# A hybrid decoder block in float32: the order of work in the second pair's mixers, and more weight sums split ahead

## The chip, the cores and the metric

One core of a Trainium2 chip. The time is device microseconds of one execution on that core, from runs of the same program; a profile of one further execution shows where it went. TensorE (PE) multiplies, VectorE (DVE), ScalarE (ACT) and GpSimd (POOL) do the rest, and DMAs are issued from the queues of SyncE (SP), ACT and POOL.

## What is computed

One layer of a decoder trunk on x of 2048 rows by 1024 columns, all in float32. The reference, cut to what matters:

```python
h = rmsnorm(x, norm_mix_g)
u = h @ w_in                       # 1024 -> 3*512 + 2*1024 columns
gate_b, gate_c, v, x_r, g = split(u)
y_conv = gate_b * causal_dwconv(gate_c * v, conv_w)          # 3 taps
xr = causal_dwconv(x_r, rnn_conv_w) + rnn_conv_b             # 4 taps
y_rnn = rg_lru(xr, w_a, b_a, w_x, b_x, lru_lambda) * gelu(g) # gates by 64x64 blocks, scan over rows
y = concat[rmsnorm(y_conv, g_norm_conv), rmsnorm(y_rnn, g_norm_rnn)]
x = x + y @ w_out                  # 1536 -> 1024
h = rmsnorm(x, norm_mlp_g)
x = x + relu(h @ w_mlp_in)**2 @ w_mlp_out                    # 1024 -> 4096 -> 1024
out = rmsnorm(x, final_norm_g)
```

## The kernel before, in words

**Pairs of blocks.** The 2048 rows are four blocks of 512. They are worked in two pairs, one after the other: mixers (the projection `w_in`, the convolutions and the recurrence), then the output projection `w_out`, then the MLP's two products, which the page calls `up` and `dn`. A pair's mixers of the first pair (`mixers_plain`) multiply plainly. Those of the second pair (`mixers_blocks`) and both MLP products (`Up`, `Down`) treat the two blocks, two halves of the inner size and two halves of the columns as a 2 by 2 matrix product and do it in seven block products in place of eight, with sums of quarters as operands. The seven products are numbered 1 to 7 and run in `ORDER = (1, 2, 6, 5, 7, 3, 4)`. Products 1, 2 and 4 take a quarter of the weights as it is; 7, 5, 6 and 3 take a sum of quarters.

**Splits.** Each operand is split in a high and a low part of the type fp32r (`round_off`: ACT casts the high part, DVE subtracts it from the source for the low part, lines 172 and 173), and a product is three passes: high by high, high by low, low by high. A block product of the mixers is 24 matmuls of 128x512 (line 885, written `in`), one of `Down` is 24 as well (line 1187, `dn`).

**The second pair's mixers.** The columns of `w_in` are seven groups, run in the order `SEQUENCE = (0, 4, 1, 5, 2, 6, 3)`. Groups 0 to 3 (`InLru`) hold the recurrence's input and its gate g, 4 and 5 (`InConv`) the convolution's c and v, 6 (`InGate`) its b. The list `seq` of 49 products starts with products 1 and 2 of the groups 0 and 4, then the other five of group 0 (n = 4 to 8) and of group 4 (n = 9 to 13), then seven each of the groups 1, 5, 2, 6 and 3 (n = 14 to 48). For each n the loop fetches the weights of a product three or four places ahead, splits (`prepare`) those that were fetched raw two places ahead, multiplies, empties PSUM (`drain`), and then does one step of the recurrence of the LRU group before, if one is due:

- step 0: the gate products of the group's first unit (`psri`, line 518), and the second unit's convolution and split (`xr`, `xr_hi`, `xr_lo`);
- step 1: the first unit's scan: a tanh and an exponential on ACT (lines 541 and 542), DVE work, a square root on ACT, the scan itself on DVE (line 548), and on POOL the copy of its last state (line 549);
- step 2: the second unit's gate products, the first unit's output;
- steps 3 and 4: the second unit's scan and its output.

`STEPS` says after which product of a group each step runs: `{1: 0, 6: 1, 5: 2, 7: 3, 3: 4}` for the groups 5 and 6, and `STEPS2` for group 4, whose products 1 and 2 run early. Group 3's steps run between the row tiles of `w_out` (`between`).

**Weight sums ahead.** The first pair's mixers store each quarter that stands as it is already split (`d_ws`, a high and a low part of 512 KB each), and each sum of quarters unsplit (`d_wk`, 512 KB). In the first pair's `Down` loop, which has 56 products (n = 0 to 55), `split_sums(k)` loads one such sum (`wk`), splits it and stores both parts. It runs at every third product, 16 times, which covers the four sums of each of the groups 0 to 3. The sums of the groups 4, 5 and 6 stay raw: in the second pair's mixers the SP queue loads each, and `prepare` splits it on ACT and DVE. What was split ahead comes through the POOL queue as two loads (`wr`, line 857) straight into two tiles that the matmuls read.

**Tiles and queues.** Weights, LRU units and raws of the mixers share one pool of 15 tiles of 128x1024 (`wtile`), most other data one of 23 (`temp`); a tile is reused when its last reader is done. PSUM has four tiles. The order on PE is the program's. The order on ACT, DVE, POOL and SP is chosen by a planner that walks the program by priority with modelled times; every queue then runs in that fixed order. `tc.issue_after(ins)` puts the instructions traced under it that are on the same engine as `ins` behind `ins` in this order.

**Between the stages.** `take` loads and splits the next unit of `w_in` or `w_out`. In group 3, `load_unit` already asks for the first `w_out` unit (`oA0`) at product 7 and the second (`oA1`) at product 3; both are split when `w_out` starts. `stats` makes the sums of squares of a whole pair with one-column matmuls into PSUM (`sps`, line 646), block by block, and the inverse roots from them. The last row tiles of the second pair are finished in an order written out by hand for PE, ACT and DVE: `end_tile` gives the tail of a tile, of which `scale()` is run after the next tile's addition and squares.

Of the kernel before, what the change touches and what calls it, by code (L numbers as in the profile page):

```python
# [8 lines left out]
F32 = mybir.dt.float32  # L9
# [5 lines left out]
P = 128  # L15
# [22 lines left out]
LEADW = 2  # L38
ORDER = (1, 2, 6, 5, 7, 3, 4)
STEPS = {1: 0, 6: 1, 5: 2, 7: 3, 3: 4}  # L40
STEPS2 = {6: 0, 5: 1, 7: 2, 3: 3, 4: 4}
GROUPS = [("x%d" % p, COL_X + 256 * p, "g%d" % p, COL_G + 256 * p) for p in range(4)]
GROUPS += [("c%d" % p, COL_C + 256 * p, "v%d" % p, COL_V + 256 * p) for p in range(2)]
GROUPS += [("b0", COL_B, "b1", COL_B + 256)]
# [17 lines left out]
def block_kernel(  # L62
# [46 lines left out]
    def psum(name, shape=(P, 2, TB)):  # L109
        return psp.tile(list(shape), F32, tag="ps", name=name)  # L110
# [12 lines left out]
    def small(name):  # L123
        return sp.tile([P, NT], F32, tag=name, name=name)

    def load(dst, src):
        queued[0] = nc.sync.dma_start(dst, src).ins

# [40 lines left out]
    cursor = [0]  # L169

    def round_off(hi, src, lo):
        nc.scalar.copy(hi, src)  # L172
        latest[0] = V.tensor_tensor(lo, src, hi.bitcast(F32), SUB).ins  # L173

    latest = [None]

    def split_new(src, new, nm):
        shape = list(src.shape)
# [139 lines left out]
    nc.scalar.activation(warm, ones[:, 0:1], AF.Sqrt)  # L318

    def rstd_of(dst, v, n):  # L320
        a = small("rs_a")[:, :n]
        s = small("rs_s")[:, :n]
        q = small("rs_q")[:, :n]
        V.tensor_scalar(a, v, 1.0 / D, EPS, MUL, ADD)
        root = nc.scalar.activation(s, a, AF.Sqrt)
        V.reciprocal(s, s)
        if n == 1:
            V.scalar_tensor_tensor(q, s, a, s, MUL, MUL)
        else:
            V.tensor_mul(q, s, s)  # L330
            V.tensor_mul(q, q, a)
        V.tensor_scalar(q, q, -0.5, 1.5, MUL, ADD)
        V.tensor_mul(dst, s, q)
        return root.ins
# [303 lines left out]
        return refill("u", d, lambda nm, shape: wide(nm))  # L638

    def stats(acc, n, nm):  # L640
        res = []
        for blk in range(2):
            ps = psum("sps", (P, NT))
            for t in range(NT):
                a = blk * TB + t * P
                nc.tensor.matmul(  # L646
                    ps[:, t : t + 1], acc[:, a : a + P], ones[:, 0:1], start=True, stop=True
                )
            ss = small("ys_" + nm)
            V.tensor_scalar(ss, ps, float(D) / n, None, MUL)  # L650
            r = small("yr_" + nm)
            rstd_of(r, ss, NT)
            res.append(r)
        return res

    def split_y(y, nm, c0):
        hi = temp("y_hi", dt=F32R)
# [25 lines left out]
            kept[n, i] = spill("wk", t, nc.gpsimd)  # L683

    def split_sums(k):
        key = (k // 4, (7, 5, 6, 3)[k % 4])
        t = refill("wk", kept[key])
        kept[key] = [spill_r("ws", r, nc.gpsimd) for r in split_new(t, temp, "w")]

# [286 lines left out]
    def mixers_blocks(H, more):  # L976
        G = [InLru(n) for n in range(4)] + [InConv(n) for n in (4, 5)] + [InGate(6)]
        two = SEQUENCE[:2]
        seq = [(n, i) for n in two for i in ORDER[:2]]
        seq += [(n, i) for n in two for i in ORDER[2:]]  # L980
        seq += [(n, i) for n in SEQUENCE[2:] for i in ORDER]
        behind = {b: a for a, b in zip(SEQUENCE, SEQUENCE[1:]) if a < 4}
        mix = Mix()

        def step(p, k):
            if k == 0:
                p.units[0].gate(p.gw)
                p.units[1].conv(p.xin)
            elif k == 1:
                p.units[0].scan()  # L990
            elif k == 2:
                p.units[1].gate(p.gw)
                mix.out(p.units[0], p.g)
            elif k == 3:
                p.units[1].scan()
            elif k == 4:
                mix.out(p.units[1], p.g)

        for n in range(-FETCHW, len(seq)):
            for m, sums in ((n + FETCHW, True), (n + FETCHW - 1, False)):  # L1000
                if 0 <= m < len(seq) and (seq[m][0] > 3 and seq[m][1] not in (1, 2, 4)) == sums:
                    G[seq[m][0]].fetch(seq[m][1])
            m = n + LEADW
            if 0 <= m < len(seq):
                G[seq[m][0]].prepare(seq[m][1])
            if n < 0:
                continue
            s, i = seq[n]
            if s == 6 and i == 1:
                G[6].us = [G[4].u, G[5].u]  # L1010
            G[s].multiply(i, H)
            G[s].drain(i)
            more(n)
            if s in behind:
                k = (STEPS2 if s == two[1] else STEPS).get(i)
                if k is not None:
                    step(G[behind[s]], k)
            if s == 6 and i in (3, 4):
                mix.conv(G[6].u0 if i == 3 else G[6].u1)
            if s == 3 and i == 6:  # L1020
                rA = stats(mix.acc["A"], 512, "A")
            if s == 3 and i in (7, 3):
                load_unit(cursor[0] + (i == 3))
            if s == 3 and i == 3:
                fetched = [fetch_y(mix.ys["A"], q, 0) for q in range(2)]

        def between(t):
            if t == 0:
                step(G[3], 0)
                step(G[3], 1)  # L1030
            if t == 1:
                step(G[3], 2)
                step(G[3], 3)
            if t == 3:
                step(G[3], 4)

        return mix, rA, conv_operands(fetched), between
# [197 lines left out]
    def end_tile(b, t, gfin, ss, final):  # L1235
        rs = small("rs")[:, 0:1]
        a = small("rs_a")[:, 0:1]
        V.scalar_tensor_tensor(a, ss[:, 0:1], 1.0 / D, ss[:, 1:2], MUL, ADD)
        root_of(rs, a)
        r0 = b * TB + t * P  # L1240
        x0, x1 = (x_half(b, t, i) for i in range(2))

        def scale():
            nc.scalar.activation(x1, x1, AF.Copy, scale=rs)  # L1244
            (nc.scalar if final else nc.sync).dma_start(outf[r0 : r0 + P, HALF[1]], x1)
            V.scalar_tensor_tensor(x0, x0, rs, gfin[:, HALF[0]], MUL, MUL)  # L1246
            nc.sync.dma_start(outf[r0 : r0 + P, HALF[0]], x0)

        return scale

    def finish(b):
        gfin = gain(final_norm_g)
# [112 lines left out]
    for b in range(0, NB, 2):  # L1365
# [99 lines left out]
        with tc.manual_schedule(engines={nc.tensor.engine}):  # L1465
# [52 lines left out]
            for n in range(len(dseq) - (0 if more else 2)):  # L1518
# [14 lines left out]
                if (i, a) == (4, 0):  # L1533
                    finish(b)
                if more:
                    if n % 3 == 2 and n < 48:
                        split_sums(n // 3)
                    if (i, a) == (5, 0):
                        load_xt(2)
                        ops2 = Operands()  # L1540
                    if (i, a) == (6, 1):
                        diags = [diagonal(rs_next[:, k, :], NT) for k in range(2)]
                    if (i, a) == (6, 4):
                        bcs = [temp("bcs", (P, TB)) for _ in range(2)]
                        for k in range(2):
                            nc.scalar.copy(bcs[k], spread(rs_next[:, k, :], NT, diags[k]))
                    if i == 7 and a < 4:
                        r0 = [xtt[2, q] for q in range(4)]
                        scale_rows(r0[a], 2 * a, bcs[0], 2)
                        ops2.first_two(1 + a // 2, r0[a])  # L1550
                    if (i, a) == (7, 4):
                        load_xt(3)
                    if i == 3 and a < 4:
                        r1 = [xtt[3, q] for q in range(4)]
                        scale_rows(r1[a], 2 * a, bcs[1], 2)
                    if i == 3 and a in (5, 6):
                        q = a - 5
                        V.tensor_tensor(r0[q], r1[q], r0[q], SUB)
                    if i == 4 and a in (0, 1):
                        if a == 0:  # L1560
                            T2 = [temp("T2") for _ in range(2)]
                        V.tensor_tensor(T2[a], r1[2 + a], r0[a], SUB)
                        V.tensor_tensor(r0[2 + a], r0[2 + a], T2[a], SUB)
                        V.tensor_tensor(r1[a], r1[2 + a], r1[a], SUB)
                    if i == 4 and a == 3:
                        ops2.put(ops2.begin(6), T2)
                    if i == 4 and a == 5:
                        ops2.put(ops2.begin(5), r0[:2])
# [8 lines left out]
        if not more:  # L1577
            order = (0, 2, 1, 3)
            with tc.manual_schedule(
# [3 lines left out]
                for t in order:  # L1583
                    for i, a in dseq[-2:]:
                        down.multiply(i, a, (t,))
                    xv = x_half(b + 1, t, 0)
                    V.tensor_add(xv, down.x[t // 2][:, t % 2], xv)  # L1587
                    finish_squares(b + 1, t, ends[t], (0,))
                    if done:
                        done()  # L1590
                    done = end_tile(b + 1, t, gfin, ends[t], t == order[-1])
                done()
        if more:
            finish(b + 1)
            ops = ops2
# [57 lines left out]
```

## Time and profile before

| | us |
|---|---|
| three runs: median (lowest to highest) | 2144.76 (2143.79 to 2151.07) |
| the profiled execution | 2144.81 |
| its span, first to last instruction | 2143.0 |
| mean granted TensorE clock in it | 0.997 |
| first pair's mixers, `w_out` | 0 to 474 |
| first pair's `up`, `dn` | 474 to 1087 |
| second pair's mixers | 1087 to 1376 |
| second pair's `w_out` | 1376 to 1524 |
| second pair's `up`, `dn` | 1524 to 2135 |
| end of the last tiles | 2135 to 2143 |

The stages are read from the starts of PE's lines in the timeline. A row of the timeline has the start, the duration, engine, line, operation, the tiles written and read, the shape, the count of merged instructions, and in brackets the idle time before it with what ended it. PE's matmuls are pipelined and their ends are modelled: the time from one start to the next tells more than the duration.

### The profile page before, as it was taken

The page shows a single profiled execution, that of the slowest core. Times are in us where ns is not written, and L with a number is a line of the kernel's source. Part 1 is how long each engine was busy: PE and PEld are TensorE (multiplying, and loading weights), DVE is VectorE, ACT ScalarE, POOL GpSimd, SP SyncE. Part 2 cuts the span into 40 slices and gives each one's busy share as a digit, 9 for nine tenths or more (in the row PEclk, how much of TensorE's full clock was granted, in tenths as well). Part 3 has the DMA queues.
Part 4 walks back from the last instruction along what each step waited for, and adds up shares of the span by engine and source line. Part 5 has one row for each costly group of instructions (what it writes and reads, how often), then busy time and mean ns, then how long its engine had stood idle before and what let it go on. Part 6 is the DMA issues. An engine that isn't in the chain of part 4 may idle for free. (4 is left out here: it accounts for less than half of the span.)

```text
span 2143.0 us, 25113 instructions
## 1 busy us (share of the span) xinstructions
PE 2122.8 (99%) x9488; PEld 1746.1 (81%) x9488; DVE 1480.4 (69%) x1726; ACT 972.0 (45%) x1224; POOL 184.3 (9%) x335
## 2 busy tenths in 40 slices
PE   9999999999999999999999999999999999999998
PEld 8888887888888888888887887778888888888887
DVE  5887877569787875576847567595886665644446
ACT  6744637354333344453536447474433233433334
POOL 1121210000111100000121121000000000000000
PEclk9999999999999999999999999999999999999999
DMA  8755754442887799699573574654144444876441
GB/s 302 290 209 209 277 189 165 152 146 104 316 307 271 283 346 408 255 405 328 177 258 121 177 267 165 238 187 167 50 167 158 157 157 175 330 293 230 158 149 79
DMA packets 180904, 472.51 MB, mean 220 GB/s; under 512 B 15664, under 2 KB 62768, under 8 KB 179760
## 3 DMA queue, kind: packets, MB, share of 16 engines
q1 hardware_dynamic: 141536, 329.08, 42.3%
q0 software_dynamic: 36800, 133.19, 16.6%
q10 hardware_dynamic: 2448, 8.65, 1.1%
q8 instruction: 74, 1.21, 0.2%
q14 instruction: 46, 0.38, 0.1%
HBM read 308.33 MB, written 162.53 MB: 220 GB/s over the span
## 5 line engine op out<-in xcount | busy, mean ns | idle before, releaser
L885 PE MATMUL up<-H,w_hi 128*128 128x512 f32 x1792 | 552.1, 389 | 0.0
L173 DVE TENSOR_TENSOR w_lo<-w,w_hi 128x1024 fp32r<-128x1024 f32 x208 | 253.3, 1222 | 274.3 <-issue 163.5
L885 PEld LDWEIGHTS up<-H,w_hi 128*128 128x128 f32 x1792 | 335.9, 188 | 69.2
L1187 PE MATMUL dn<-w_hi,z_hi 128*128 128x512 f32 x896 | 349.0, 389 | 0.0
L1187 PE MATMUL dn<-w_lo,z_hi 128*128 128x512 f32 x896 | 348.8, 389 | 0.0
L885 PE MATMUL up<-H,w_lo 128*128 128x512 f32 x896 | 348.6, 389 | 0.0
L1187 PE MATMUL dn<-w_hi,z_lo 128*128 128x512 f32 x896 | 348.6, 389 | 0.0
L172 ACT CAST z_hi<-z 128x1024 fp32r<-128x1024 f32 x112 | 118.0, 1054 | 255.4 <-PE dn L1187 240.3
L172 ACT CAST w_hi<-w 128x1024 fp32r<-128x1024 f32 x208 | 215.9, 1049 | 27.0 <-DVE w L1066 13.8
L885 PE MATMUL in<-H,wr 128*128 128x512 f32 x888 | 203.1, 390 | 0.6 <-ACT g L907 0.6
L1187 PEld LDWEIGHTS dn<-w_lo,z_hi 128*128 128x128 f32 x896 | 168.2, 188 | 35.8 <-DVE w_lo L173 0.8
L885 PEld LDWEIGHTS up<-H,w_lo 128*128 128x128 f32 x896 | 168.2, 188 | 35.2
L1187 PEld LDWEIGHTS dn<-w_hi,z_hi 128*128 128x128 f32 x896 | 168.2, 188 | 35.1 <-ACT z_hi L172 0.2
L1187 PEld LDWEIGHTS dn<-w_hi,z_lo 128*128 128x128 f32 x896 | 168.2, 188 | 34.9
L885 PEld LDWEIGHTS in<-H,wr 128*128 128x128 f32 x888 | 166.4, 188 | 36.2 <-ACT g L907 1.0
L173 DVE TENSOR_TENSOR z_lo<-z,z_hi 128x1024 fp32r<-128x1024 f32 x112 | 136.6, 1219 | 22.7 <-ACT z_hi L172 21.4
L1080 ACT COPY snap<-up 128x1024 f32<-128x1024 f32 x48 | 48.7, 1016 | 177.1 <-PE up L885 177.1
L258 PE MATMUL po<-w_hi,y_hi 128*128 128x512 f32 x384 | 122.0, 399 | 4.7 <-ACT w_hi L172 3.0
L258 PE MATMUL po<-w_lo,y_hi 128*128 128x512 f32 x384 | 119.8, 394 | 0.2 <-DVE w_lo L173 0.2
L258 PE MATMUL po<-w_hi,y_lo 128*128 128x512 f32 x384 | 119.9, 394 | 0.0
L172 ACT CAST w_hi<-raw 128x1024 fp32r<-128x1024 f32 (+1 forms) x62 | 62.8, 1020 | 84.3 <-PE ps_x L235 25.0
L173 DVE TENSOR_TENSOR w_lo<-raw,w_hi 128x1024 fp32r<-128x1024 f32 (+1 forms) x62 | 73.3, 1186 | 39.2 <-issue 20.3
(275 smaller groups left out, 3095.0 us busy)
## 6 DMA issues: line engine op xcount, KB each, us to landing
z<-d_z SPq DMA_DIRECT2D x112, 512.0 KB, 7.4
w<-in_w_mlp_out_dram SPq DMA_DIRECT2D x80, 512.0 KB, 6.0
wr<-d_ws POOLq DMA_DIRECT2D x74, 512.0 KB, 6.4
w<-in_w_mlp_in_dram SPq DMA_DIRECT2D x64, 512.0 KB, 4.8
d_z<-snap SPq DMA_DIRECT2D x64, 512.0 KB, 3.0
w<-d_w SPq DMA_DIRECT2D x64, 512.0 KB, 4.7
d_z<-z SPq DMA_DIRECT2D x48, 512.0 KB, 3.0
d_ws<-w_hi POOLq DMA_DIRECT2D x37, 512.0 KB, 6.6
```

What stands on the lines that cost most here:

```text
L172: nc.scalar.copy(hi, src)
L173: latest[0] = V.tensor_tensor(lo, src, hi.bitcast(F32), SUB).ins
L258: nc.tensor.matmul(ps[:, half, :], ys[:, j, t * P : (t + 1) * P], ws[j][:, 0, half * 512 : (half + 1) * 512], start=first and i == 0, stop ...
L885: nc.tensor.matmul(ps[:, j, :], ws[:, k, j * P : (j + 1) * P], hs(k), start=i in (1, 2, 5) and k == 0 and n == 0, stop=k == 3 and n == len ...
L1080: nc.scalar.copy(t, ps)
L1187: nc.tensor.matmul(ps[t // 2][:, t % 2, :], zs[:, p, t * P : (t + 1) * P], ws[:, p, :], start=i in (1, 2, 5) and a == 0 and p == 0 and n == 0,
```

## The change

Five edits:

- `STEPS2` moves the steps of group 0's recurrence by one product: steps 0 to 3 after the products 5, 7, 3 and 4 of group 4, step 4 after the first product of group 1 (n = 14).
- Each step of the mixers is issued behind the latest cast (`cast[0]`) that was traced when the iteration's `prepare` was done.
- `split_sums` runs at every second product of the first pair's `Down`, 28 times, and takes the groups in the order `SEQUENCE`: the sums of all seven groups are split ahead.
- In group 3, `oA0` is loaded at product 6 and split at product 7; `oA1` is loaded at product 3 as before.
- `stats` writes both blocks into one PSUM tile and does the small DVE work once for eight columns; `scale()` is cut in two, the ACT half before the next tile's addition, the DVE half where it was.

```diff
-STEPS2 = {6: 0, 5: 1, 7: 2, 3: 3, 4: 4}
+STEPS2 = {5: 0, 7: 1, 3: 2, 4: 3}
...
     def round_off(hi, src, lo):
-        nc.scalar.copy(hi, src)
+        cast[0] = nc.scalar.copy(hi, src).ins
...
     def rstd_of(dst, v, n):
-        a = small("rs_a")[:, :n]
-        s = small("rs_s")[:, :n]
-        q = small("rs_q")[:, :n]
+        new = small if n <= NT else pair
+        a, s, q = (new("rs_%s%d" % (c, n > NT))[:, :n] for c in "asq")
...
     def stats(acc, n, nm):
-        res = []
-        for blk in range(2):
-            ps = psum("sps", (P, NT))
-            for t in range(NT):
-                a = blk * TB + t * P
-                nc.tensor.matmul(
-                    ps[:, t : t + 1], acc[:, a : a + P], ones[:, 0:1], start=True, stop=True
-                )
-            ss = small("ys_" + nm)
...
+        ps = psum("sps", (P, 2 * NT))
+        for t in range(2 * NT):
+            nc.tensor.matmul(
+                ps[:, t : t + 1], acc[:, t * P : t * P + P], ones[:, 0:1], start=True, stop=True
+            )
+        ss = pair("ys_" + nm)
+        V.tensor_scalar(ss, ps, float(D) / n, None, MUL)
+        r = pair("yr_" + nm)
+        rstd_of(r, ss, 2 * NT)
+        return [r[:, :NT], r[:, NT:]]
...
     def split_sums(k):
-        key = (k // 4, (7, 5, 6, 3)[k % 4])
+        key = (SEQUENCE[k // 4], (7, 5, 6, 3)[k % 4])
...
                 G[seq[m][0]].prepare(seq[m][1])
+                split = [cast[0]]
...
                 if k is not None:
-                    step(G[behind[s]], k)
+                    with tc.issue_after(split[0]):
+                        step(G[behind[s]], k)
+            if n == 14:
+                step(G[two[0]], 4)
...
-            if s == 3 and i in (7, 3):
-                load_unit(cursor[0] + (i == 3))
+            if s == 3 and i == 6:
+                load_unit(cursor[0])
+            if s == 3 and i == 7:
+                split_unit(cursor[0])
+            if s == 3 and i == 3:
+                load_unit(cursor[0] + 1)
...
-        def scale():
+        def upper():
             nc.scalar.activation(x1, x1, AF.Copy, scale=rs)
             (nc.scalar if final else nc.sync).dma_start(outf[r0 : r0 + P, HALF[1]], x1)
+
+        def lower():
             V.scalar_tensor_tensor(x0, x0, rs, gfin[:, HALF[0]], MUL, MUL)
             nc.sync.dma_start(outf[r0 : r0 + P, HALF[0]], x0)
...
-                    if n % 3 == 2 and n < 48:
-                        split_sums(n // 3)
+                    if n % 2:
+                        split_sums(n // 2)
...
+                    if done:
+                        done[0]()
                     xv = x_half(b + 1, t, 0)
                     V.tensor_add(xv, down.x[t // 2][:, t % 2], xv)
                     finish_squares(b + 1, t, ends[t], (0,))
                     if done:
-                        done()
+                        done[1]()
```

More of the change, by code (lines that the diff above doesn't have):

```diff
@@ L124, in small, with pair @@
         return sp.tile([P, NT], F32, tag=name, name=name)
+    def pair(name):
+        return sp.tile([P, 2 * NT], F32, tag=name, name=name)
     def load(dst, src):
@@ L171, in round_off @@
     def round_off(hi, src, lo):
-        nc.scalar.copy(hi, src)
+        cast[0] = nc.scalar.copy(hi, src).ins
         latest[0] = V.tensor_tensor(lo, src, hi.bitcast(F32), SUB).ins
     latest = [None]
+    cast = [None]
     def split_new(src, new, nm):
@@ L640, in stats @@
     def stats(acc, n, nm):
-        res = []
-        for blk in range(2):
-            ps = psum("sps", (P, NT))
-            for t in range(NT):
-                a = blk * TB + t * P
-                nc.tensor.matmul(
-                    ps[:, t : t + 1], acc[:, a : a + P], ones[:, 0:1], start=True, stop=True
-                )
-            ss = small("ys_" + nm)
[L650 to L654, printed above, removed]
+        ps = psum("sps", (P, 2 * NT))
[8 more added lines that the diff above has]
+        return [r[:, :NT], r[:, NT:]]
     def split_y(y, nm, c0):
@@ L1241, in end_tile @@
         x0, x1 = (x_half(b, t, i) for i in range(2))
-        def scale():
+        def upper():
             nc.scalar.activation(x1, x1, AF.Copy, scale=rs)
             (nc.scalar if final else nc.sync).dma_start(outf[r0 : r0 + P, HALF[1]], x1)
+        def lower():
             V.scalar_tensor_tensor(x0, x0, rs, gfin[:, HALF[0]], MUL, MUL)
             nc.sync.dma_start(outf[r0 : r0 + P, HALF[0]], x0)
-        return scale
+        return upper, lower
     def finish(b):
@@ L1589, in block_kernel @@
                     if done:
-                        done()
+                        done[1]()
                     done = end_tile(b + 1, t, gfin, ends[t], t == order[-1])
-                done()
+                for part in done:
+                    part()
         if more:
```

## The prediction

> **What bounds the kernel now.** I read the page first, then the windows by stage, then PE's waits and its timeline where PE had stood still.
>
> ```profile
> PE 2122.8 (99%) x9488; PEld 1746.1 (81%) x9488; DVE 1480.4 (69%) x1726; ACT 972.0 (45%) x1224; POOL 184.3 (9%) x335
> ```
>
> TensorE is the bound: 20.2 us of the 2143.0 us span (2143.0 - 2122.8) are all that it stands idle, and the change adds and removes no large matmul. The windows show where a part of this lies, and that DMA is the second resource to watch (the columns end with the granted clock, the DMA share and GB/s).
>
> ```profile
> 781.00:1087.00 306.00, 306.00 (x1346) 252.39 (x1346) 202.51 (x214) 142.10 (x162) 27.26 (x51) 1.00 0.85 319
> 785.00:985.00 200.00, 200.00 (x879) 164.63 (x878) 136.03 (x131) 94.65 (x96) 13.87 (x26) 1.00 0.92 357
> 985.00:1087.00 102.00, 102.00 (x451) 84.46 (x450) 63.24 (x81) 43.59 (x63) 13.40 (x25) 1.00 0.69 243
> 800.00:850.00 50.00, 50.00 (x223) 41.39 (x222) 29.79 (x26) 22.53 (x23) 4.81 (x9) 1.00 1.03 409
> 1087.00:1373.00 286.00, 281.35 (x1266) 228.14 (x1265) 182.89 (x198) 149.44 (x161) 53.20 (x88) 1.00 0.59 206
> ...
> 1370.00:1380.00 10.00, 6.78 (x23) 4.76 (x22) 8.57 (x9) 6.53 (x7) 0.00 (x0) 0.79 0.00 1
> 1380.00:1390.00 10.00, 10.00 (x44) 7.58 (x44) 5.73 (x7) 3.48 (x4) 0.00 (x0) 0.87 0.61 211
> ```
>
> The first pair's second MLP product (first row, 56 block products, so 5.46 us each) has no idle PE at all. The second pair's mixers lose 4.65 us (286.00 - 281.35). The start of `w_out` behind them loses 3.2 us, and the clock there is granted at 0.79 and 0.87, which is another (0.21 + 0.13) x 10 = 3.4 us. So the change can win only in a few places, and it loads the first pair's second product, which runs without a gap now.
>
> **The change part by part.**
>
> *Group 4's steps.* PE's starts around the second gate product:
>
> ```profile
> 1143.54 0.73 PE L885 MATMUL in<-H,w_hi 128*128 128x512 f32 x2
> ...
> 1144.11 0.39 PE L885 MATMUL in<-H,w_lo 128*128 128x512 f32 x1
> ...
> 1154.83 0.51 PE L518 MATMUL psri<-xr_hi,gate 64*128 64x512 f32 x2
> 1156.28 0.50 PE L518 MATMUL psri<-xr_lo,gate 64*128 64x512 f32 x2 [0.95 <-DVE xr_lo L173]
> 1156.62 0.62 PE L518 MATMUL psri<-xr_hi,gate 64*128 64x512 f32 x4
> ...
> 1157.64 0.73 PE L885 MATMUL in<-H,w_hi 128*128 128x512 f32 x2
> 1159.15 0.50 PE L885 MATMUL in<-H,w_lo 128*128 128x512 f32 x1 [0.77 <-DVE w_lo L173]
> ```
>
> From `xr_hi` to `xr_lo` PE took 1.45 us where 0.34 us does (the next pair of starts): 1.11 us lost. From `w_hi` to `w_lo` it took 1.51 us where the undisturbed place at the top took 0.57: 0.94 us lost. The second goes because the sum's split is no longer done here. For the first, ACT and DVE:
>
> ```profile
> 1150.05 1.28 DVE L504 SCALAR_TENSOR_TENSOR xr<-xr_in,prm,xr 128x1024 f32<-128x1024 f32 x1
> ...
> 1152.68 1.15 ACT L542 ACTIVATE r<-r,sp 128x1024 f32<-128x1024 f32 x1
> 1153.74 1.04 ACT L172 CAST xr_hi<-xr 128x1024 fp32r<-128x1024 f32 x1
> ```
>
> The second unit's convolution ended at 1151.33, but its cast stands behind the first unit's scan on ACT (its exponential, line 542, and the table load before it) and ran at 1153.74, 2.4 us later. In the new order `cast[0]`, when step 1 is traced, is this very cast, so the scan's ACT work goes behind it; 2.4 us earlier is more than the 1.11 us that PE waited. The distance from step 0 to step 2 stays two products. I take 1.11 + 0.94 = 2.05 us, between 0.94 (the order comes out no better) and 2.05. The scan ends some 2 us later against PE for that, and its successors move a product back; all of it lies beside block products whose PSUM tiles have been emptied, with the next group's steps seven products away. That is its cover; without it each late `drain` would stop PE by about its length, 1 us.
>
> *Groups 5 and 6.* Their raw sums collide with step 1 in the same way:
>
> ```profile
> PE in L885 <- DVE w_lo L173: 1.5, 3, 0.8
> ...
> 1305.98 0.39 PE L885 MATMUL in<-H,w_lo 128*128 128x512 f32 x1
> 1307.88 0.73 PE L885 MATMUL in<-H,w_hi 128*128 128x512 f32 x2 [1.51 <-ACT w_hi L172]
> 1309.14 0.50 PE L885 MATMUL in<-H,w_lo 128*128 128x512 f32 x1 [0.52 <-DVE w_lo L173]
> ```
>
> 1.90 us in place of 0.23 (306 us by 1344 matmuls), then 1.26 in place of 0.57: 2.36 us. The third of the three waits, in group 5, is 1.5 - 0.77 - 0.52 = 0.2 us. Both go: 2.6 us. In their place POOL issues 24 more `wr` loads of 512 KB, 12.6 MB, where SP issued 12 raw ones; at a DMA share of 0.59 in this stage there is room. What may be late next is the queue, below.
>
> *The start of `w_out`.*
>
> ```profile
> 1373.45 1.02 ACT L918 ACTIVATE g<-in 128x1024 f32<-128x1024 f32 x1 [8.91 <-PE in L885]
> 1374.37 1.04 ACT L172 CAST xr_hi<-xr 128x1024 fp32r<-128x1024 f32 x1
> 1375.31 3.88 ACT L172 CAST w_hi<-raw 128x1024 fp32r<-128x1024 f32 x4
> ...
> 1376.58 4.62 DVE L173 TENSOR_TENSOR w_lo<-raw,w_hi 128x1024 fp32r<-128x1024 f32 x4
> ...
> 1376.41 1.22 PE L258 MATMUL po<-w_hi,y_hi 128*128 128x512 f32 x2 [2.99 <-ACT w_hi L172]
> 1377.86 1.22 PE L258 MATMUL po<-w_lo,y_hi 128*128 128x512 f32 x2 [0.23 <-DVE w_lo L173]
> ```
>
> ACT stood idle for 8.91 us, and then did the casts of both units behind the last drain. With `oA0` split at product 7, two of the four casts go into that idle time: 2.99 + 0.23 us of waits go, and with them, I think, the 3.4 us of low clock that begin at this stop. `oA1` stays behind the drain. Its first cast would run at 1375.3 to 1376.3, its first low part, 1.2 us (4.62 / 4), behind xr's, at 1376.5 to 1377.7; PE, having no wait now, needs them after 12 matmuls of 0.23 us, at 1373.4 + 2.7 = 1376.1 and 1376.7. So 0.2 + 1.0 = 1.2 us come back. Net 3.2 + 3.4 - 1.2 = 5.4 us, between 2.0 (the clock falls all the same) and 6.6.
>
> *`stats`.*
>
> ```profile
> PE sps L646 <- DVE ys_B L650: 0.9, 2, 0.6
> ```
>
> The second block's matmuls waited for the PSUM tile that the first block's sums held. With one tile this wait goes in both pairs: 0.9 us, between 0.5 (DVE, which was late for the longer one, is late for the next wait instead) and 1.1. The small DVE work that falls away was beside PE.
>
> *The tail.*
>
> ```profile
> 2129.80 0.69 DVE L1587 TENSOR_TENSOR x<-dn,x 128x512 f32<-128x512 f32 x1
> ...
> 2131.15 0.71 ACT L1244 ACTIVATE x<-x,rs 128x512 f32<-128x512 f32 x1
> ...
> 2132.71 0.69 DVE L1587 TENSOR_TENSOR x<-dn,x 128x512 f32<-128x512 f32 x1
> ...
> 2134.81 0.39 PE L1187 MATMUL dn<-w_hi,z_lo 128*128 128x512 f32 x1
> ...
> 2135.61 0.68 DVE L1587 TENSOR_TENSOR x<-dn,x 128x512 f32<-128x512 f32 x1
> ```
>
> Each tile takes 2.91 us on this chain, with the ACT scaling between its squares and its root. The scaling moves beside the addition. The root then starts when DVE's small step behind the squares is done, about 0.3 us earlier; 2.6 us are less than PE's 12 matmuls (2.73 us). So the last addition starts at PE's end, 2135.2, 0.4 us earlier, and its own tail is 0.3 us shorter: 0.7 us.
>
> *The sums ahead.* Twelve more in the first pair's second product, each 0.52 MB read and 1.05 MB written:
>
> ```profile
> DMA packets 29912, 97.66 MB, mean 319 GB/s; under 512 B 3036, under 2 KB 3036, under 8 KB 29895
> ...
> ACT z_hi L172 <- PE dn L1187: 82.8, 30, 4.1
> ...
> ACT z_hi L172 <- DMA z<-d_z: 10.2, 3, 5.9
> ```
>
> 18.9 MB more, 116.6 MB in 306 us, 381 GB/s, where 409 was held for 50 us. In the loaded part, 785 to 985, 19 sums are due in place of 12: 7 x 1.57 MB at 409 GB/s are 27 us of DMA, where (1 - 0.92) x 200 = 16 us are free. So DMA falls some 11 us behind by 985, and catches up after, where 31% of 102 us are free. Against that, ACT's casts of z waited 30 times for PE to free a tile and 3 times for data: operands are ready ahead of PE by about the two products of the program's lead. ACT (142 us of 306) and DVE (203) take 12 more casts of 1.04 us (as `xr_hi` above) and subtractions of 1.2 us easily. I cost it at nothing, with up to 2 us for a late split as the upper end.
>
> The sum: 2.05 + 2.6 + 5.4 + 0.9 + 0.7 = 11.6 us off the profiled execution's 2144.81 us (span 2143.0 and 1.8 around it; the median of the runs, 2144.76, is the same): **2133.2 us**.
>
> [...]
>
> **The rivals.**
>
> *DMA becomes the bound of the first pair's second product (slower).* For it: 785 to 985 ran at share 0.92 and 357 GB/s, and if this mix of packets under 8 KB, reads and writes can hold no more over the whole stage, 116.6 MB take 326.6 us, 20.6 us over the 306. PE then waits for z and w. It decides from the point at which the lag outgrows the lead of two products, 10.9 us, which is what I worked out for 985. Against it: 409 GB/s over 50 us. Time: 2133.2 + 20.6 = 2153.8, slower than before. [...]
>
> *The POOL queue takes the place of the raw splits.* The state copies stand in the same fixed queue as the 24 new loads, and each waits for a scan; loads wait for tiles.
>
> ```profile
> ACT xr L558 <- POOL state L549: 9.3, 3, 7.2
> ```
>
> Once ACT already waited 7.2 us behind it without PE noticing. If such a stop falls on a `wr` or a drain that PE needs, 7.2 us come back: 2140.4. Against it: loads run two to three products ahead.
>
> *The planner leaves `oA0`'s casts behind the drain* (tiles of the pool not yet free at product 7), so that this part does not do what it says: the 5.4 us stay, 2138.6.
>
> *All residues go too:* `oA1`'s 1.2 us, a low-clock stretch of the first pair (0.99 of 130 us, over 300 to 430 us) and a 0.6 us wait of group 3 for a copy of g:
>
> ```profile
> 300.00:430.00 130.00, 128.32 (x581) 105.04 (x580) 92.06 (x143) 68.07 (x88) 3.62 (x7) 0.99 0.42 145
> ...
> PE in L885 <- ACT g L907: 0.6, 1, 0.6
> ```
>
> 1.2 + 1.3 + 0.6 = 3.1: 2130.1.
>
> **How the numbers follow.** Forecast 0.52 (2131 to 2136; with every term at its worse end 0.94 + 2.6 + 2.0 + 0.5 + 0.7 - 2.0 = 4.7 us are left, 2140.1), `oA0` unchanged 0.16, POOL 0.14, residues 0.12, DMA 0.06. The range runs from 2129.8 to 2140.5, past the POOL rival; outside lie DMA and the edges of the others. What a measurement of this kernel can tell from no change is about 0.5%, 10.7 us, so faster means below 2134.1 and slower above 2155.5. Of the forecast's 0.52 some two thirds lie below 2134.1, with the residues' 0.12 that is 0.47; slower gets 0.03, the part of the DMA rival in which another gain fails with it; within 0.5% the rest, 0.50.
>
> **What would show it.** Right: no `w_hi` or `w_lo` waits of PE under `in`; the `xr_hi` cast ahead of the scan's tanh in group 4; two `w_hi` casts from `raw` in the ACT gap before `w_out`, PE starting there without a stop and at clock 1.00; one `sps` wait for each pair; additions in the tail 2.7 us apart. Wrong: PE waits under `dn` between 785 and 1087 (DMA), `wr` landing late behind a state copy (POOL), or the stop before `po` still there.

## The result and the profile after

| | before | changed |
|---|---|---|
| median of the runs (lowest to highest) | 2147.07 (2143.79 to 2151.07), 6 runs | 2135.80 (2132.14 to 2137.85), 6 runs |
| ratio, 95% interval | 1 | 0.9946 (0.9935 to 0.9958) |
| profiled execution, its span | 2144.81, 2143.0 | 2137.24, 2135.2 |

The change takes 11.3 us off the medians, 0.54% (0.42 to 0.65 by the interval), and 7.8 us off the two profiled spans. The forecast was 2133.2 us, in a range of 2129.8 to 2140.5. The stages, from one start of PE's lines to the next (us); the column "again" is a second profile of the changed kernel, unaltered, from the experiments below:

| stage | before | changed | again |
|---|---|---|---|
| first mixers | 330.51 | 330.57 | 329.60 |
| first `w_out` | 143.79 | 144.70 | 143.04 |
| first `up` | 306.53 | 307.44 | 306.52 |
| first `dn` | 306.63 | 307.46 | 306.74 |
| second mixers, with the stop ahead of `w_out` | 288.95 | 279.81 | 279.78 |
| second `w_out` | 147.20 | 146.45 | 146.33 |
| second `up` | 306.52 | 306.52 | 306.52 |
| second `dn`, end | 312.91 | 312.26 | 312.31 |

The gain sits in the second mixers: 9.1 us. PE's waits in the changed kernel over the whole run (us in total, times, longest):

```profile
PE po L262 <- DVE x L1268: 2.0, 1, 2.0
...
PE psri L521 <- DVE xr_lo L176: 0.8, 1, 0.8
PE po L262 <- DVE w_lo L176: 0.8, 1, 0.8
PE po L262 <- DVE ys_B L650: 0.8, 2, 0.5
PE dn L1194 <- DVE w_lo L176: 0.8, 1, 0.8
PE up L884 <- DVE snap L1108: 0.6, 1, 0.6
...
PE po L262 <- ACT w_hi L175: 0.3, 1, 0.3
PE in L884 <- ACT xr_in L903: 0.2, 1, 0.2
```

Every wait of `in` for a part of a weight is gone, and so is the 3.0 us stop. The remaining `psri` wait is the one that group 3's second unit already had inside `w_out`. New against before are the first line (0.7 then), the 0.8 and 0.3 us of `po` for the second unit's parts, and the short waits of `dn` and `up`.

Around the second gate product in group 4, PE and ACT:

```profile
1162.79 0.50 PE L521 MATMUL psri<-xr_hi,gate 64*128 64x512 f32 x2
1163.12 0.40 PE L521 MATMUL psri<-xr_lo,gate 64*128 64x512 f32 x2
```

```profile
1159.98 1.05 ACT L175 CAST xr_hi<-xr 128x1024 fp32r<-128x1024 f32 x1 [2.95 <-DVE xr L507]
1161.12 1.16 ACT L544 ACTIVATE xr<-r,sp 128x1024 f32<-128x1024 f32 x1
```

The cast now runs ahead of the scan's work, and PE goes from `xr_hi` to `xr_lo` in 0.33 us where it took 1.45. The start of `w_out`, ACT first, then PE:

```profile
1350.29 1.05 ACT L175 CAST w_hi<-raw 128x1024 fp32r<-128x1024 f32 x1 [8.56 <-DMA raw<-in_w_out_dram]
...
1353.38 1.05 ACT L175 CAST w_hi<-raw 128x1024 fp32r<-128x1024 f32 x1
...
1370.18 1.03 ACT L917 ACTIVATE g<-in 128x1024 f32<-128x1024 f32 x1 [8.50 <-PE in L884]
1371.10 1.04 ACT L175 CAST xr_hi<-xr 128x1024 fp32r<-128x1024 f32 x1
1372.04 1.99 ACT L175 CAST w_hi<-raw 128x1024 fp32r<-128x1024 f32 x2
```

```profile
1369.98 0.62 PE L262 MATMUL po<-w_hi,y_hi 128*128 128x512 f32 x2
...
1372.25 0.61 PE L262 MATMUL po<-w_hi,y_lo 128*128 128x512 f32 x2
1373.14 0.73 PE L262 MATMUL po<-w_hi,y_hi 128*128 128x512 f32 x2 [0.27 <-ACT w_hi L175]
1374.64 0.73 PE L262 MATMUL po<-w_lo,y_hi 128*128 128x512 f32 x2 [0.77 <-DVE w_lo L176]
```

The first unit's two casts run 17 to 20 us ahead of its first matmul. The second unit's run behind the last drain, and PE meets them after 12 matmuls: 0.89 in place of 0.45 us to 1373.14, then 1.50 in place of 0.46, so 1.5 us come back. The windows of the first `dn`, the second mixers, and the clock around `w_out` (the columns end with the granted clock, the DMA share and GB/s):

```profile
783.00:1090.00 307.00, 306.25 (x1348) 252.71 (x1347) 217.32 (x227) 153.46 (x174) 38.08 (x72) 1.00 0.96 370
787.00:987.00 200.00, 199.25 (x875) 164.06 (x874) 133.08 (x126) 98.21 (x101) 19.25 (x36) 1.00 0.98 381
...
1090.00:1370.00 280.00, 279.75 (x1267) 228.54 (x1266) 171.95 (x181) 138.31 (x149) 68.67 (x116) 1.00 0.71 243
...
1365.00:1375.00 10.00, 8.95 (x39) 6.80 (x38) 8.41 (x8) 4.80 (x5) 0.00 (x0) 1.00 0.35 139
...
351.60:355.00 3.40, 3.40 (x8) 2.64 (x9) 3.40 (x3) 2.27 (x3) 0.18 (x1) 0.50 0.41 137
1430.30:1433.60 3.30, 3.19 (x8) 2.54 (x9) 2.27 (x6) 3.15 (x6) 0.00 (x0) 0.50 0.31 102
```

PE is idle for 0.25 us of the second mixers' 280, where it was 4.65 of 286. The first `dn` runs at 381 GB/s over 200 us and loses under 1 us. The clock stays at 1.00 at the start of `w_out`, but a stretch at 0.50 stands behind the statistics at 1430, and another in the first `w_out`.

### The profile page after: what moved, and what is told of

Same layout as the page of the kernel before. It is cut to its first block, busy times and chain, and to the rows that moved or that the text cites. A ratio compares the mean times of both kernels' runs of the same rounds, so it can differ in the third digit from the quotient of the medians.

```text
span 2135.2 us, 25168 instructions
## 1 busy us (share of the span) xinstructions
PE 2120.2 (99%) x9488; PEld 1746.1 (82%) x9488; DVE 1479.2 (69%) x1698; ACT 970.4 (45%) x1219; POOL 210.6 (10%) x383
## 5 line engine op out<-in xcount | busy, mean ns | idle before, releaser
L884 PE MATMUL in<-H,wr 128*128 128x512 f32 x1176 | 269.1, 390 | 0.2 <-ACT xr_in L903 0.2
L884 PEld LDWEIGHTS in<-H,wr 128*128 128x128 f32 x1176 | 220.2, 188 | 48.2 <-issue 2.2
```

Source lines behind the costliest of these rows:

```text
L884: nc.tensor.matmul(ps[:, j, :], ws[:, k, j * P : (j + 1) * P], hs(k), start=i in (1, 2, 5) and k == 0 and n == 0, stop=k == 3 and n == len ...
```

## The experiments

Beside each variant, the kernel before ran again on the same chip; ratios are to it. The variants ran on three chips, so they are compared with each other by stages and by ratios. "Mixers" means the second pair's, up to the first matmul of `w_out`. Each run has its mean granted clock beside it; (1 - clock) times the span is the time that this run lost to a lower clock. It averages 8.0 us over the 40 runs of the kernel before that stand beside the variants, and 3.9 us over the 11 runs of the changed kernel.

**The convolution groups' sums left raw again.**

```diff
-        key = (SEQUENCE[k // 4], (7, 5, 6, 3)[k % 4])
+        key = (k // 4, (7, 5, 6, 3)[k % 4])
...
-                    if n % 2:
-                        split_sums(n // 2)
+                    if n % 3 == 2 and n < 48:
+                        split_sums(n // 3)
```

> The changed kernel with the sums of before: 16 split ahead at every third product of the first pair's dn, those of the groups 4, 5 and 6 split in the second pair's mixers. Theory (the splits collided with the recurrence's steps): PE waits under in for w_hi and w_lo are back in the groups 5 and 6, about 2.6 us, and in group 4 up to 0.9 us; the second pair's mixers, from the first in to the first po, 279.8 us in the changed kernel, take 282 to 284. Rival (the moved steps and the order behind the cast removed those waits): the mixers stay at 280. In both the first pair's dn loses its wait of 0.8 us for w_lo at 789 us or keeps it; DMA share of the first pair's dn falls from 0.96 to about 0.85.

Measured: 2139.01 us, ratio 0.9972 (0.9962 to 0.9983); mixers 282.84 us, 3.0 more than with the change. PE's waits:

```profile
PE in L884 <- ACT w_hi L175: 2.0, 1, 2.0
...
PE in L884 <- DVE w_lo L176: 0.7, 2, 0.5
```

So the raw sums' splits are 3.0 us of the mixers' gain, nearly all in group 6, where two starts come 2.2 and 0.7 us late. By the ratios (0.9972 against 0.9946 and, further below, 0.9937) they are worth 5.6 to 7.5 us; the clock is a part of the rest, with 6.4 us lost to it on average over the nine runs, 2.5 more than in the changed kernel. In group 4, with the moved steps, the raw split holds nothing up: the 0.9 us that it cost there before has two cures as well.

**The steps behind group 4 in their old places.**

```diff
-STEPS2 = {5: 0, 7: 1, 3: 2, 4: 3}
+STEPS2 = {6: 0, 5: 1, 7: 2, 3: 3, 4: 4}
...
-            if n == 14:
-                step(G[two[0]], 4)
```

> The changed kernel with the steps of group 0's recurrence back in their old places (step 0 after product 6 of group 4, and so on), everything else of the change kept, so that all weight sums still come already split. Theory A (the splits of the sums were what collided with the steps; where the steps stand matters little): the second pair's mixers, from the first projection matmul to the first of w_out, stay within 0.5 us of the changed kernel's 279.81 us, and no wait of the projection's matmuls is over 0.3 us. Rival B (my prediction's 1.11 us: the gate product of group 4 waited for the second unit's low part because of the place of the steps): the wait for the low part is back at about 1 us and the mixers are 1.0 to 1.3 us longer.

Measured: one run, 2135.67 us; mixers 279.71 us, and `xr_lo` 0.34 us behind `xr_hi`. The old places cost nothing here.

**The steps not held behind the latest cast.**

```diff
-                    with tc.issue_after(split[0]):
-                        step(G[behind[s]], k)
+                    step(G[behind[s]], k)
```

> The changed kernel without the order behind the cast. Theory: the scan's tanh and exponential of group 0 stand ahead of the second unit's xr_hi cast again, and PE waits about 1.1 us for xr_lo at group 4's second gate product; mixers 281 us in place of 279.8. Rival (with the raw splits gone the planner puts the cast first by itself, or the moved steps do it): no such wait, 279.8 us.

Measured: 2134.75 us, ratio 0.9948 (0.9934 to 0.9961); mixers 279.90 us, no wait back. So neither of the two edits on the steps is needed while the other stands. The next kernel is without both.

**Only the sums.** The kernel before, with the change's two lines on `split_sums` and nothing else.

> The kernel before with one edit: the sums of all seven groups split ahead at every second product of the first pair's second MLP product; steps, w_out's units, stats and tail as before. Theory A: the four waits of the projection's matmuls for a high or low part of a weight (2.1 + 1.5 + 0.8 + 0.4 us in the kernel before) go, the gate product's wait of about 1 us may stay, and so does the stop of about 3 us ahead of w_out: 284 to 286 us from the first projection matmul to the first of w_out, where the kernel before has 288.95, so 3 to 5 us of the second pair's mixers are the sums' own. Rival B (the sums help only together with the moved steps): 288 us or more. The first pair's second MLP product stays at 306.5 to 307.5 us by both.

Measured: one run, 2144.39 us; mixers 284.39 us, 4.6 less than before. In its timeline the gate product of group 4 is late as it was (PE, then ACT):

```profile
1154.64 0.51 PE L518 MATMUL psri<-xr_hi,gate 64*128 64x512 f32 x2
1156.09 0.50 PE L518 MATMUL psri<-xr_lo,gate 64*128 64x512 f32 x2 [0.95 <-DVE xr_lo L173]
```

```profile
1152.49 1.15 ACT L542 ACTIVATE r<-r,sp 128x1024 f32<-128x1024 f32 x1
1153.55 1.04 ACT L172 CAST xr_hi<-xr 128x1024 fp32r<-128x1024 f32 x1
```

So the sums alone don't cure it: the cast `xr_hi` still stands behind the scan's exponential. In the changed kernel either edit on the steps is enough to keep this wait of 1.1 us away, and here, with neither, it stays. This kernel also lacks the edits on `w_out`, `stats` and the tail. They stand at other places of the program, but no run took the two edits on the steps alone out of the changed kernel, so that these others have no part in the cure is argued, not shown. Over the whole span little is left of the 4.6 us (2141.2 for 2143.0): the stop ahead of `w_out` is still there, and the second `w_out` takes 150.07 us, 2.9 more, with half-clock stretches of 3.41 and 6.83 us and a wait of 1.7 us under `sps`.

**The first unit of `w_out` loaded and split as before.**

```diff
-            if s == 3 and i == 6:
-                load_unit(cursor[0])
-            if s == 3 and i == 7:
-                split_unit(cursor[0])
-            if s == 3 and i == 3:
-                load_unit(cursor[0] + 1)
+            if s == 3 and i in (7, 3):
+                load_unit(cursor[0] + (i == 3))
```

> The changed kernel with the first unit of the output projection loaded at product 7 and split only when the output projection starts. Theory: PE stands about 3.2 us at the first po of the second pair and the clock falls to half behind it for 3.4 to 6.8 us; against the 1.4 us of waits that the changed kernel has there, 3.5 to 5.2 us more in all. Rival (the low clock is not tied to this stop): only 1.8 us more.

Measured: 2141.92 us, ratio 0.9981 (0.997 to 0.9991).

```profile
PE dn L1190 <- DVE w_lo L176: 4.0, 1, 4.0
PE po L262 <- ACT w_hi L175: 3.0, 1, 3.0
```

The stop is back and mixers are 282.96 us, 3.15 more; a half-clock stretch of 3.41 us began at 1377.96, behind the stop and a second wait of 0.72 us, and `w_out` took 147.96. That makes 4.7 us by these two stages of one profile, where the medians are 6.1 apart. The runs show the rest: the 12 of this variant lost 7.1 us to the clock on average and the 11 of the changed kernel 3.9. So some 3.2 us of clock (standard error 0.6) come back with the 3.15 us of the stop, 6.4 in all, more than the 3.5 to 5.2 us that were expected. The 4.0 us wait of `dn` lies at 787 us, far ahead of the edit's place; whether it would come again, no second profile of this variant shows.

**The statistics block by block again**, by the old `stats` and `rstd_of`:

```diff
     def stats(acc, n, nm):
-        ps = psum("sps", (P, 2 * NT))
-        for t in range(2 * NT):
+        res = []
+        for blk in range(2):
+            ps = psum("sps", (P, NT))
+            for t in range(NT):
...
```

> The changed kernel with stats block by block and its roots as before. Theory (the fewer small DVE instructions made the planner put a row addition of the first pair behind the scan): the 2.0 us wait of po for that addition at 351 us is 0.7 us again, and the sps waits of 0.9 us are back: about 0.4 us faster or the same. Rival (the order changed for another reason): the 2.0 us stay and 0.9 us are lost.

Measured: 2136.28 us, ratio 0.996 (0.9945 to 0.9975).

```profile
PE sps L650 <- DVE ys_B L654: 2.6, 2, 2.3
...
PE po L262 <- DVE x L1273: 0.7, 1, 0.7
```

Both sides show: the `sps` waits are back and the second `w_out` takes 148.59 us, 2.1 more; the row addition's wait in the first pair falls from 2.0 to 0.7 us and the first `w_out` takes 143.80, 0.9 less (each stage has one half-clock stretch in both kernels). The size of the first is not this code's alone: the longest `sps` wait is 2.3 us here, 1.7 in "only the sums" and 0.6 in the kernel before, all with the same `stats`. By the ratios (0.9960 against 0.9946 and 0.9937, with intervals that overlap) the kernel tends to be slower without the merge, where the same time or a little less was expected. In the changed kernel a row addition that DVE did at 344.34 before had slid behind the splits of y and other work, to 348.91:

```profile
348.91 0.75 DVE L1268 SCALAR_TENSOR_TENSOR x<-po,yr_A,x 128x512 f32<-128x512 f32 x1
...
350.71 0.75 DVE L1268 SCALAR_TENSOR_TENSOR x<-po,yr_A,x 128x512 f32<-128x512 f32 x1
```

**Where DMA binds.** Each split sum stored twice; the copy is never read.

```diff
-        kept[key] = [spill_r("ws", r, nc.gpsimd) for r in split_new(t, temp, "w")]
+        parts = split_new(t, temp, "w")
+        kept[key] = [spill_r("ws", r, nc.gpsimd) for r in parts]
+        for r in parts:
+            spill_r("ws2", r, nc.gpsimd)
```

> The changed kernel with every split sum stored twice in the first pair's second MLP product: 28 times 1.05 MB, 29.4 MB more beside the 113.3 MB that the profile counts there, so about 143 MB; the second copy is never read. If the DMAs of this core can hold 409 GB/s, as they did for 50 us, over the whole stage, it takes about 350 us where 307.5 were taken, and TensorE waits in it for about 40 us. [...] If the mean of 370 GB/s of the changed kernel was set by demand alone and the DMAs can do much more, the stage stays under 315 us. Elsewhere nothing changes.

Measured: one run, 2187.55 us; the first `dn` takes 349.53 us. PE's waits and a window inside the stage:

```profile
PE dn L1197 <- DVE w_lo L176: 26.4, 10, 5.1
PE in L887 <- DMA wr<-d_ws: 9.4, 1, 9.4
```

```profile
800.00:1100.00 300.00, 274.51 (x1142) 221.47 (x1141) 176.92 (x189) 128.44 (x147) 53.21 (x101) 0.95 1.01 403
```

The expected 350 us came out: with the DMA share at 1.01, this mix moved 403 GB/s. Of the 42 us that the stage takes more, 27.4 are waits under `dn` (1.0 of them for another part of DVE's work) and 13.7 are lost to half clock, in eight lengths of 3.41 us. The DMA view of the changed kernel for this stage (783 to 1090) says:

```profile
DMA packets 34326, 113.73 MB, mean 370 GB/s; under 512 B 3529, under 2 KB 3529, under 8 KB 34308
```

At 403 GB/s these 113.73 MB take 282 us, so 25 us of DMA time (10 MB) are free on average. The 9.4 us are the POOL queue's: the next pair's first loads wait there behind the stores.

**The changed kernel again**, unaltered, and after it two kernels that go on from it.

> The changed kernel itself once more, unaltered, for a second profile of it and its time on the same chip as the next kernel. Theory: the waits that its program fixes are there again (about 2.0 us in the first pair's w_out for the row addition, 0.8 and 0.3 us for the second weight unit and 0.8 us for the gate product in the second pair's w_out), while the short waits of the first pair's two MLP products (0.6 and 0.8 us) and the half-clock stretches in the first and second w_out come out at other sizes or other places, since three variants with the same program there had none of the former. Rival: they are there again at the same places and sizes, and so belong to the change. Ratio to the kernel before 0.994 to 0.996.

Measured: 2133.23 us (2130.94 to 2134.53), ratio 0.9937 (0.9924 to 0.9949), span 2130.8.

```profile
PE po L262 <- DVE x L1268: 2.0, 1, 2.0
...
PE psri L521 <- DVE xr_lo L176: 0.8, 1, 0.8
PE po L262 <- DVE w_lo L176: 0.8, 1, 0.8
```

```profile
346.00:356.00 10.00, 8.03 (x36) 6.33 (x35) 10.00 (x12) 8.00 (x8) 0.18 (x1) 1.00 0.59 173
...
1422.00:1432.00 10.00, 9.74 (x45) 8.07 (x44) 8.89 (x17) 5.09 (x7) 0.00 (x0) 0.83 0.79 268
```

The waits that the program fixes are the same to a tenth. The waits of `up` and `dn` and the half-clock stretch of the first `w_out` are not there (the clock is 1.00 in the first window above), and the stretch behind the statistics is (0.83 in the second): the two spans of one program differ by 4.4 us, of which 1.0 + 1.7 + 0.9 + 0.7 lie in the first four stages of the table. So the first pair's losses in the first profile are mostly not the change's. The second profile puts the gain at 2143.0 - 2130.8 = 12.2 us, the first at 7.8, and the medians, 11.3 and 12.7, are the better measure. Two things came out otherwise than expected: the ratio is just under the 0.994 to 0.996, and the stretch behind the statistics is at the same place again.

**Cover for the second unit.** In the second pair's first `w_out`, two row tiles take the first unit before either takes the second, and group 3's steps 2 and 3 run a tile later.

```diff
-             if t == 1:
+             if t == 2:
...
+                if (t, pr) == (1, 0) and b == 2:
+                    continue
+                for u in (0, 1) if b == 2 and (t, pr) == (0, 0) else (t,):
+                    if pr == 0:
+                        pos[u] = psum("po")
+                    for j in range(2):
+                        mm_rows(pos[u], ys[pr], ws[pr], j, u, pr == 0 and j == 0, pr == 1 and j == 1)
+            add_rows(b, t, pos[t], r)
```

> The changed kernel with two edits in the second pair's first w_out: its first two row tiles both take the first weight unit before either takes the second, so that the second unit's split, which runs behind the last drain, has 24 matmuls of cover in place of 12; and group 3's steps 2 and 3 run after the third row tile in place of the second, so that the gate product finds its low part ready. Theory: the two waits at the start of w_out for the second unit (0.8 + 0.3 us) and the gate product's wait (0.8 us) go, so the second pair's w_out falls by about 2 us from 146.45 us and the ratio to the kernel before is about 0.9935. Rival: the later steps end the last recurrence late and another wait of the same size appears at the statistics behind w_out or at the second block's row tiles: 146.0 us or more, ratio 0.9946 or above.

Measured: 2132.27 us (2128.92 to 2133.27), ratio 0.9937 (0.9924 to 0.9951). The whole list of PE's waits:

```profile
PE po L262 <- DVE x L1268: 1.9, 1, 1.9
PE start_x L438 <- POOL ones L273: 1.1, 1, 1.1
PE po L262 <- DVE ys_B L650: 0.8, 2, 0.5
PE po L262 <- ACT gi L535: 0.5, 1, 0.5
```

The three waits are gone and the second `w_out` takes 142.20 us: 4.25 less than the changed kernel, of which 1.7 are a half-clock stretch that this profile lacks and 2.5 the edit. The ratio is 0.9937, as for the changed kernel run again on another chip, so the stage shows this gain and the times do not.

**The same, with the first pair's statistics of the convolution half made block by block.**

```diff
-                    rA = stats(mix.acc["A"], 512, "A")
+                    rA = stats_blocks(mix.acc["A"], 512, "A")
```

> The kernel with the first two row tiles of the second pair's first w_out taken together (and group 3's steps 2 and 3 a tile later), with one more edit: the first pair's statistics for the convolution half are made block by block again, as before the change, and all others stay in one tile. Theory (the merged form let a row addition of the first pair slide behind other work of the vector engine): TensorE's longest wait for a row addition falls from 1.9 to 0.7 us, the first pair's w_out from 143.05 to about 141.8 us (with no half-clock stretch in either), and the time falls by 1.2 us against that kernel's 2132.27, to about 2131; ratio near 0.993. Rival: the wait moves to the statistics or to the second unit's row tiles, and w_out stays at 143 us.

Measured: 2130.77 us (2127.55 to 2134.71), ratio 0.9927 (0.9912 to 0.9943).

```profile
PE po L262 <- DVE ys_B L666: 0.8, 2, 0.5
PE po L262 <- DVE x L1284: 0.7, 1, 0.7
```

The addition's wait is 0.7 us and the first `w_out` 141.76, 1.3 less than in the kernel that it starts from. On the same chip the changed kernel had 2133.23: 2.5 us more by the medians, where the two edits' stages give 2.5 + 1.3 = 3.8. The runs of the two overlap (2127.55 to 2134.71 against 2130.94 to 2134.53), so the medians show the sign better than the size.

## Why the prediction held, step by step

- **Group 4's steps** (2.05 us). The gate product's start and the weight's low part took 1.1 and 0.9 us less, as worked out. The named cause, the cast behind the scan, is what "only the sums" shows. Not seen ahead: the moved places alone would have done it, so the edit that I argued from is one of two sufficient ones.
- **Groups 5 and 6** (2.6 us). Right; leaving these sums raw, and group 4's with them, cost 3.0 us, nearly all in these two groups.
- **The mixers' sum** came out at 9.1 us where 4.65 + 2.99 = 7.6 were priced. The waits of a view are less than what a stop costs: behind the stops the next step between starts is longer too (0.34 us from 1159.15 to 1159.49 and 0.33 from 1309.14 to 1309.47 in the kernel before, where 0.23 is the mean of the first `dn`), the gate product itself had started 0.2 us late, and the wait for a copy of g, put among the residues, went while one of 0.2 us came.
- **The start of `w_out`** (3.2 + 3.4 - 1.2). The stop went, shown by undoing it. The second unit gave 1.5 us back for 1.2. The 3.4 us of low clock were read from two windows of one profile. By the profiles alone the term looks mis-sized: at this place the low clock did go, but a stretch at half clock, 1.7 us, stood 60 us later behind the statistics in both profiles of the changed kernel, and the profile of before has three lengths of 3.41 us (two of them in one stretch), those of the changed kernel two and one. Over the runs the term holds: undoing this edit brings back some 3.2 us of clock, and the whole change takes 8.0 - 3.9 = 4.1 us of it away. That one profile gave so near a size is luck, since the stretches differ from one execution to the next (last section).
- **`stats`** (0.9 us). Right for the waits on `sps` (none is left, where one for each pair was named), wrong as a sum. "The small DVE work that falls away was beside PE" left out that a planner orders that work anew: in the first pair an addition slid and cost 1.3 us; in the second pair, undoing the merge cost 2.1 us. Against before, the waits of the first profile sum to a loss: 0.9 us gone, 1.3 (addition) and 0.3 (`ys_B`, which the second profile lacks) come.
- **The tail** (0.7 us). The last additions after the change:

```profile
2122.61 0.69 DVE L1598 TENSOR_TENSOR x<-dn,x 128x512 f32<-128x512 f32 x1
2125.34 0.69 DVE L1598 TENSOR_TENSOR x<-dn,x 128x512 f32<-128x512 f32 x1
2128.05 0.69 DVE L1598 TENSOR_TENSOR x<-dn,x 128x512 f32<-128x512 f32 x1
```

  They are 2.72 us apart, PE's pace. From the start of `dn` to the end it is 312.26 for 312.91 us: 0.65, and "only the sums", which has the old tail, takes 312.92.
- **The sums ahead** at nothing, and the DMA rival at 0.06. Storing twice shows where the bound stands: 403 GB/s, with 25 us left. The 357 GB/s from which the rival worked out its 20.6 us are no limit here: 381 were held over 200 us in the changed kernel and 403 over 300 us with the double stores. How close the slack is, is open: `dn` waited up to 0.8 us for a low part in one profile of the changed kernel (a sign that the prediction had put under "wrong") and not at all in the other, and 4.0 us in one variant, but also 0.7 us in the variant with the old 16 sums. Whether 28 sums make such waits likelier can't be told from one profile of each.
- **The other rivals.** POOL: the state copies held ACT for 6.7 us in the second pair's mixers and PE for none; its queue became a wait only with twice the stores. The first unit did not stay behind the drain.

The time came out 2.6 us above the forecast in the first runs (2135.80) and on it in the second set (2133.23). The kernel before came out 2.3 us above the three runs that the forecast starts from; as a ratio the forecast is 0.9946, and so is the first measurement. The same sum with the terms of the profiles, 1.7 for the clock in place of 3.4, 1.5 for the second unit, -0.7 for `stats` and 1.5 more for the mixers, gives 2.05 + 2.6 + 3.2 + 1.7 - 1.5 - 0.7 + 0.7 + 1.5 = 9.6 us, 2135.3. With the 4.1 us of clock that the runs show it gives 12.0, where the medians fell by 11.3 and 12.7. Beside the 11.6 forecast, the mixers gave 1.5 us and the clock 0.7 more, `stats` 1.6 and the second unit 0.3 less: errors of opposite sign nearly cancel, and that the sum is so close is in part luck.

## What to carry to other kernels

A wait of the bound engine that comes from one in-order queue (a cast behind a scan, a split behind a drain) is cured by taking the work out of that queue or by putting it earlier in the cover, and the trace prices it within a few tenths where one wait is read by itself (2.05 and 2.6 us here); look at starts, not at waits, for the whole price. Small work that is merged or dropped beside the bound engine is not free of effect where a planner orders the queues: check which instruction slid. Profile the same program twice before a difference of a few microseconds in one stage is put down to an edit, and price the clock by the mean granted clock of all runs, not by the stretches of one profile.

## What the hardware showed unexpectedly

A stretch at half clock lasted 3.41 us, cost 1.7 us (144.70 against 143.04 us for one stage of the same program) and came with pauses that were shorter than it. In the first profile of the changed kernel:

```profile
1428.07 1.84 PE L646 MATMUL sps<-ones,xr 128*128 128x1 f32 x16
1430.41 1.22 PE L262 MATMUL po<-w_hi,y_hi 128*128 128x512 f32 x2 [0.50 <-DVE ys_B L650]
```

Sixteen one-column matmuls and a wait of 0.50 us, 2.34 us together, and the clock was at 0.50 from 1430.3 to 1433.6. The length of the pause does not decide alone. In the kernel before, the same sixteen matmuls with their waits took 2.85 us in the second `w_out`, and the clock stayed at 1.00:

```profile
1436.27 0.95 PE L646 MATMUL sps<-ones,xr 128*128 128x1 f32 x8
1437.82 1.05 PE L646 MATMUL sps<-ones,xr 128*128 128x1 f32 x8 [0.60 <-DVE ys_B L650]
1439.12 0.73 PE L258 MATMUL po<-w_hi,y_hi 128*128 128x512 f32 x2 [0.26 <-DVE ys_B L650]
```

Pauses of three profiles, with the clock in a window at or behind them (statistics: from the first one-column matmul to the next of 512 columns; in the second profile of the changed kernel the longest wait alone):

| profile | pause | clock, in the window (us) |
|---|---|---|
| before | statistics, 2.51 us, from 385.69 | 0.50, 389.40 to 392.80 |
| before | stop ahead of the second `w_out`, wait of 3.0 us | 0.50, 1375.90 to 1382.70 |
| before | statistics, 2.85 us, from 1436.27 | 1.00, 1436.00 to 1443.00 |
| changed | row addition, wait of 2.0 us | 0.50, 351.60 to 355.00 |
| changed | statistics, 2.10 us, from 388.62 | 1.00, 388.60 to 394.50 |
| changed | statistics, 2.34 us, from 1428.07 | 0.50, 1430.30 to 1433.60 |
| again | row addition, wait of 2.0 us | 1.00, 346.00 to 356.00 |
| again | statistics in the second `w_out`, wait of at most 0.3 us | 0.83, 1422.00 to 1432.00 |

Nor does a stretch have to begin where PE goes on: in the first row PE took up its 512-column matmuls again at 388.20, without a further wait, and the clock was 1.00 from 388.00 to 389.40. The 2.0 us wait of one program, for the row addition, was followed by a stretch in one execution and by none in the other, so a stretch of one profile need not come in the next. The 3.0 us stop has one at it in the kernel before and in the variant with the late first unit (3.41 us, from 1377.96). What decides it is not shown here. One more stretch, left out of the counts above, stands at the very end, behind the last matmuls: the clock is 0.68 from 2139 to 2143 in the kernel before and 0.80 from 2131 to 2135 in the changed one, with no matmul in either window.
